# One more seven-product pair per group, more transfers that add, and an instruction order computed by the kernel, in a streaming-encoder layer

## The chip, the cores and the metric

The kernel runs on one core of a Trainium2 chip. The metric is device microseconds (us) of one execution. PE is the engine for matmuls, DVE the vector engine, ACT the one for activations, POOL and SP issue transfers (POOL those that add to what stands at the destination).

## The reference

One layer on 256 tokens of width 2048, all in float32:

```python
x = x + 0.5 * swiglu(rms_norm(x, ffn1_norm), ffn1_w_up, ffn1_w_down)      # D_FF = 5632
proj = rms_norm(x, mix_norm) @ w_in                                      # columns: q f i g, x_b gate_b, gates
y_a = HGRN2 recurrence over (q, f, i), chunkwise, normed, times silu(g)  # 8 heads of 128
y_b = causal conv(4) -> RG-LRU scan, times gelu(gate_b)
x = x + (sigmoid(gate_A) * (y_a @ w_branch_a) + sigmoid(gate_B) * (y_b @ w_branch_b)) @ w_out
x = x + cross_attention(rms_norm(x), rms_norm(mem))                      # 4 heads, 256 memory tokens
x = x + 0.5 * swiglu(rms_norm(x, ffn2_norm), ffn2_w_up, ffn2_w_down)
return rms_norm(x, final_norm)
```

## The kernel before, in words

Every float32 product is made of three: each operand is split into a high part (ACT copies it, rounded, to `h`) and a low part (DVE subtracts, to `l`; `split`, L119), and PE adds high x high, low x high and high x low into one bank of accumulators (`three`, L448). The stationary operand of a matmul is a 128 x 128 piece of activations, the moving one a stretch of weights of 512 (or 256) columns. Weights come as pieces of 128 x 2048, each brought by SP into one of three `raw` buffers and prepared by `prepare` (L195) into one of three `h` and three `l` buffers. One list, `plan`, gives the order of all pieces; `weights` (L165) prepares two pieces ahead.

A feed-forward network (`ffn`, L467) runs over 11 groups of 512 hidden columns. A group takes 8 pieces of up weights, one per pair p of activation blocks, then up to 4 pieces of down weights of earlier groups. A pair's piece holds a 2 x 2 block product, and there are three kinds:

- plain: 8 block products, 24 matmuls of 512 columns; the weights are split as they are.
- fast: 7 block products instead of 8 (a scheme of sums and differences), 21 matmuls. `prepare` makes three differences of the weights on DVE (`td`, L213 to L215), splits three quarters of the piece (`l`, 128 x 1536) and the differences (`tl`, twice 128 x 1024).
- mixed: 8 block products on the sums that the fast pairs of the same group need, 24 matmuls, weights split as in plain. With the kind "added" the low part is made without DVE (`begin_added`, L186): SP brings the piece into the only `own` buffer, ACT writes its negated high part into `l` (L191), and POOL issues a transfer from `own` that adds to `l` (L192).

`ffn_order` (L42) fixes the order: in groups 3 to 10 the pairs go 1, 3, 0, 4, 2, 6, 5, 7, pairs 0 and 6 mixed (added, but for pair 0 of group 3) and the six others fast; the down pieces, plain, follow. At a group's end DVE and ACT gather the accumulators into `ev`, PE turns them by transposes (L491), and they become `hidop`.

In the middle, a generator (`hgrn`, L752) does the recurrence beside the projections: `pump` takes a step or two from it after each projection product. Its small matmuls (`blocks`, L763, from L768, and L788) have 32 or 64 stationary columns instead of 128, and are built 32, 16 or 8 at a time.

The order on each engine is worked out by the framework's scheduler from program order and priorities; only the first pieces are put in order by hand (`in_turn`, L165 to L182), and `tc.issue_after` holds a few groups back.

Of the kernel before, what the change touches and what calls it, by code (L numbers as in the profile page):

```python
# [2 lines left out]

# [10 lines left out]
P = 128  # L14
# [27 lines left out]
def ffn_order():  # L42

    out, down = [("plain", 0, p) for p in range(8)], [("down", 0, 1, c, 0) for c in range(4)]
    for g in range(1, NG):
        if g < 3:  # L50
            out += [(("mixed", "fast")[p % 2], g, p) for p in (0, 1, 2, 3, 5, 4, 7, 6)]
        else:
            out += [("mixed" if p in (0, 6) else "fast", g, p) for p in (1, 3, 0, 4, 2, 6, 5, 7)]
        if g > 2 and g % 2:
            down = [("down", g - 2, 2, c, b) for c in range(4) for b in (g - 2, g - 1)]
        n = 2 if g < 3 else 4
        out, down = out + down[:n], down[n:]
    return out + [("down", NG - 2, 2, c, b) for c in range(4) for b in (NG - 2, NG - 1)]


@with_exitstack
def block_kernel(ctx: ExitStack, tc: tile.TileContext, xT, xin, memT, vec, gfin, bgate, lruw, wu1, wd1, win, wv,
                 wg, wab, wout, wq, wk, wvm, wo, wu2, wd2, out_):
    nc = tc.nc
    pe, dve, act, sp = nc.tensor, nc.vector, nc.scalar, nc.sync

    def pool(name, bufs, **kw):
        return ctx.enter_context(tc.tile_pool(name=name, bufs=bufs, **kw))

# [9 lines left out]
    @contextmanager  # L79
    def scope(**pools):  # L80
        with ExitStack() as inner:
            for name, bufs in pools.items():
                scoped[name] = inner.enter_context(tc.tile_pool(name=name, bufs=bufs, reuse_waits="tile"))
            yield
            scoped.clear()

# [75 lines left out]
    planned = count()  # L162
    in_turn = ExitStack()
# [22 lines left out]
    def begin_added(src):  # L186

        raw = scoped["own"].tile([P, 2048], F32, name="own", tag="own")
        l = lp.tile([P, 2048], F32R, name="l", tag="l")
        sp.dma_start(raw, src)  # L190
        act.activation(l, raw, ACT.Copy, scale=-1.0)  # L191
        nc.gpsimd.dma_start(l, raw, accum_op=ALU.add)  # L192
        return raw, l
# [145 lines left out]

    FFN_POOLS = dict(wide=3, own=1)  # L340

# [62 lines left out]

    BOTH = [2, 4]
    xd = []

    def operand_pairs(src, gain, q, xg, out):

        for a in src:  # L410
# [8 lines left out]
            if 2 * q + i in BOTH:  # L419
                if 2 * q + i == BOTH[0]:  # L420
                    xd.append(slot(F32R, "xd"))
                n = 512 * BOTH.index(2 * q + i)
                less = [xd[-1][:, a:a + 256] for a in (n, n + 256)]
            out.append(((h, l), less))

        def sums(which=((0, "less"), (0, "sums"), (1, "less"), (1, "sums"))):
            s = slot(name="xs")
            for i, ((h, l), less) in enumerate(out):
                a = [xg[:, i * 512 + j * P:][:, :P] for j in range(4)]

                def made(h, l, n, at, terms):
# [3 lines left out]
                    split(h, l, s[:, at:at + n * P])  # L435

                if less and (i, "less") in which:
                    made(*less, 2, 0, lambda o: ((a[0], a[1], ALU.subtract), (a[2], a[3], ALU.subtract)))
# [28 lines left out]
    def ffn(name, pairs, sq, then, begin=(), sums=(), rstds=()):  # L467
# [39 lines left out]
        for at, e in enumerate(order):  # L507
# [3 lines left out]
            if kind != "down":  # L511
# [13 lines left out]
                if ends or last:  # L525
                    if ends or kind == "plain":
# [4 lines left out]
                        if rstd is None:  # L531
                            with tc.issue_after(done["high"]):
                                rstd = sq.rstd_tokens()
                if ends:
# [115 lines left out]
    def to_mix(c, t):  # L650
# [3 lines left out]
        if c == 0:  # L654
            with tc.issue_after(done["residual"]):
                parameters()
        if c == 2:
# [94 lines left out]
    def hgrn(hf):  # L752
# [10 lines left out]
        def blocks(acc, n, pick):  # L763
            for i in range(8):
                g, h = divmod(i, 4)
                for b in range(0, P, 32):
# [6 lines left out]
                          in1=col("eye", 0, 32)[:, None, :].broadcast_to([P, 8, 32]), op=ALU.mult)  # L773
        nc.gpsimd.memset(S[:, :1024], 0.0)
        yield
# [320 lines left out]

    with scope(**FFN_POOLS):
        ffn("ffn2", pairs2, sq4, to_out, late, sums2)


# [91 lines left out]
```

## Time and profile before

| | us |
|---|---|
| median of 3 runs (2442.12 to 2442.47) | 2442.3 |
| the profiled execution | 2442.24 |
| its span on the core | 2440.5 |
| PE busy | 2430.0 |
| DVE busy | 1892.8 |
| ACT busy | 1390.8 |
| PE's waits in all | 1.4 |
| one late group of the second network | 62.09 |

Busy is time in which an engine runs an instruction. Matmuls overlap in the records, so the sum of their durations is more than the time; what one costs is read from its start to the next start. The profile's row for a group of matmuls gives the first start and the time to the end of the last one. Small matmuls and products of plain float32 have two records each.

### The profile page before, as it was taken

Reading aid. Unit: us, or ns where it says so; the run is one execution under the profiler, and the core shown is the slowest. Engines: PE = TensorE matmul, PEld = TensorE weight load, DVE = VectorE, ACT = ScalarE, POOL = GpSimd, SP = SyncE. Lnnn points to the kernel's source line nnn. Section 1 sums busy time; section 2 is a strip of 40 time slices with the busy share of each in tenths; the row PEclk is TensorE's granted clock in tenths of the full one; section 3 lists DMA queues with packets and bytes.
Section 4 is the critical chain, followed back from the end, with each engine's and each line's share of the span. In section 5 each row is a group of like instructions: output and inputs, shape, how many; then the busy total and the mean of one; then the engine's idle time right before and its main releaser. Section 6 shows DMA issues by size and latency. Waiting matters only on the chain.

```text
span 2440.5 us, 30183 instructions
## 1 busy us (share of the span) xinstructions
PE 2430.0 (100%) x12250; PEld 2033.8 (83%) x12250; DVE 1892.8 (78%) x2016; ACT 1390.8 (57%) x1398; POOL 28.3 (1%) x36
## 2 busy tenths in 40 slices
PE   9999999999999999999999999999999999999998
PEld 8888888888888888888888888888888888888887
DVE  6999999999765757577565676556589999999995
ACT  8566666666554454477435554555555666666664
POOL 0000000000000000000000000000000000000000
PEclk9999999999999999999999999999999999999999
DMA  8557777677555545445555555544555677777763
GB/s 296 207 204 243 255 234 236 234 241 239 200 181 192 180 173 179 176 171 217 191 189 186 206 196 190 190 173 155 189 191 185 232 238 234 234 239 241 237 216 151
DMA packets 75020, 507.59 MB, mean 208 GB/s; under 512 B 8320, under 2 KB 8576, under 8 KB 15232
## 3 DMA queue, kind: packets, MB, share of 16 engines
q1 hardware_dynamic: 69840, 473.06, 53.3%
q0 software_dynamic: 4320, 31.46, 6.7%
q8 instruction: 96, 1.57, 0.2%
q10 hardware_dynamic: 720, 1.13, 0.1%
q14 instruction: 44, 0.36, 0.0%
HBM read 472.07 MB, written 2.10 MB: 194 GB/s over the span
## 4 chain that ended last, share of the span: by engine, by line
PE 97%; DVE 1%; ACT 1%; DMA 1%; issue 0%; SPq 0%; ACTq 0%; DVEq 0%
PE acc L451 18%; PE acc L454 18%; PE acc L452 18%; PE acc L231 11%; PE acc L252 8%; PE acc L253 8%; PE acc L255 8%; PE acc L235 6%; PE acc L491 1%; PE acc L391 1%; ACT h L120 0%; PE acc L768 0%; DVE l L121 0%; DMA xf<-xT 0%; PE acc L1051 0%; PE acc L1006 0%
## 5 line engine op out<-in xcount | busy, mean ns | idle before, releaser
L121 DVE TENSOR_TENSOR l<-raw,h 128x2048 fp32r<-128x2048 f32 (+2 forms) x422 | 877.9, 2087 | 364.8 <-ACT h L120 354.7
L120 ACT ACTIVATE h<-raw 128x2048 fp32r<-128x2048 f32 (+2 forms) x422 | 736.7, 1752 | 615.1 <-PE acc L253 206.2
L451 PE MATMUL acc<-h,xh 128*128 128x512 f32 x1280 | 499.0, 391 | 0.4 <-ACT h L120 0.3
L452 PE MATMUL acc<-h,xl 128*128 128x512 f32 x1280 | 496.9, 389 | 0.0
L120 ACT ACTIVATE h<-td 128x1024 fp32r<-128x1024 f32 x224 | 229.7, 1056 | 177.0 <-PE acc L452 130.8
L252 PE MATMUL acc<-h,ops 128*128 128x512 f32 x832 | 326.9, 393 | 0.0
L253 PE MATMUL acc<-h,ops 128*128 128x512 f32 x832 | 324.3, 390 | 0.0
L121 DVE TENSOR_TENSOR tl<-td,h 128x1024 fp32r<-128x1024 f32 x224 | 267.4, 1220 | 31.6 <-ACT h L120 29.0
L451 PEld LDWEIGHTS acc<-h,xh 128*128 128x128 f32 x1280 | 240.3, 188 | 53.2 <-ACT h L120 3.4
L452 PEld LDWEIGHTS acc<-h,xl 128*128 128x128 f32 x1280 | 240.3, 188 | 49.4
L231 PE MATMUL acc<-ops,h 128*128 128x512 f32 x1152 | 277.9, 393 | 0.2
L451 PE MATMUL acc<-h,hidop 128*128 128x512 f32 x704 | 275.7, 392 | 0.0
L452 PE MATMUL acc<-h,hidop 128*128 128x512 f32 x704 | 274.3, 390 | 0.0
L231 PEld LDWEIGHTS acc<-ops,h 128*128 128x128 f32 x1152 | 211.9, 188 | 42.8 <-DVE ops L292 0.9
L454 PE MATMUL acc<-l,xh 128*128 128x512 f32 x832 | 218.3, 389 | 0.0
L255 PE MATMUL acc<-l,ops 128*128 128x512 f32 x832 | 206.1, 390 | 0.0
L454 PE MATMUL acc<-l,hidop 128*128 128x512 f32 x704 | 188.3, 389 | 0.0
L255 PEld LDWEIGHTS acc<-l,ops 128*128 128x128 f32 x832 | 156.2, 188 | 32.4
L454 PEld LDWEIGHTS acc<-l,xh 128*128 128x128 f32 x832 | 156.0, 188 | 32.5
L252 PEld LDWEIGHTS acc<-h,ops 128*128 128x128 f32 x832 | 156.3, 188 | 32.3
L253 PEld LDWEIGHTS acc<-h,ops 128*128 128x128 f32 x832 | 156.3, 188 | 31.6
L454 PEld LDWEIGHTS acc<-l,hidop 128*128 128x128 f32 x704 | 132.2, 188 | 27.5
(220 smaller groups left out, 2347.9 us busy)
## 6 DMA issues: line engine op xcount, KB each, us to landing
raw<-wu SPq DMA_DIRECT2D x142, 1024.0 KB, 4.8
raw<-wd SPq DMA_DIRECT2D x88, 1024.0 KB, 4.8
raw<-win SPq DMA_DIRECT2D x40, 1024.0 KB, 4.8
raw<-wg SPq DMA_DIRECT2D x32, 1024.0 KB, 4.8
own<-wu SPq DMA_DIRECT2D x30, 1024.0 KB, 5.4
l<-own POOLq DMA_DIRECT2D x30, 1024.0 KB, 7.7
raw<-wab SPq DMA_DIRECT2D x16, 1024.0 KB, 4.8
raw<-wout SPq DMA_DIRECT2D x16, 1024.0 KB, 4.8
```

What stands on the lines that cost most here:

```text
L120: done["high"] = act.activation(h, raw, ACT.Copy).ins
L121: dve.tensor_tensor(out=l, in0=raw, in1=h.bitcast(F32), op=ALU.subtract)
L231: pe.matmul(acc, h[:, k * P:(k + 1) * P], xs[k], start=k == 0, stop=False)
L235: done["product"] = pe.matmul(acc[:, :T], l[:, k * P:(k + 1) * P], xs[k][:, :T], start=False, stop=k == KT - 1).ins
L252: pe.matmul(accs[t], x[:, t * P:][:, :P], h[j], start=first and j == 0, stop=False)
L253: pe.matmul(accs[t], x[:, T + t * P:][:, :P], h[j], start=False, stop=False)
L255: done["product"] = pe.matmul(accs[t], x[:, t * P:][:, :P], l[j], start=False, stop=last and j == 3).ins
L391: pe.transpose(accs[m // 2][:, m % 2 * T + t * P:][:, :P], tile[:, t * 512 + m * P:][:, :P], ident)
L451: pe.matmul(acc, ah, bh, start=start, stop=False)
L452: pe.matmul(acc, al, bh, start=False, stop=False)
L454: pe.matmul(acc, ah, bl, start=False, stop=stop)
L491: pe.transpose(acc[:, z * T + t * P:][:, :P], hid[t][:, (2 * y + z) * P:][:, :P], ident)
```

## The change

Three things change at once.

First, in groups 3 to 10 of both networks pair 0 becomes fast, so that only pair 6 is mixed; the order of the pairs becomes 1, 3, 0, 6, 4, 2, 5, 7. The sums for pair 0's activations are made too (`BOTH` gets a 0), in a buffer of a new pool `third`.

Second, of the down pieces that stand in groups 3 to 10, two of the four per group become "added".

Third, the kernel no longer issues its instructions to the framework as it goes. Queue objects record every operation with what it reads and writes (in cells of a tile); `price` gives each a duration; `arrange` walks through a model of the five engines, three times, and at each free engine takes the ready operation that is due first, PE's among them; and `emit` issues all in that order with the framework's scheduler off. Buffers of a pool are taken in program order where there are eight or fewer.

```diff
@@ ffn_order
-            out += [("mixed" if p in (0, 6) else "fast", g, p) for p in (1, 3, 0, 4, 2, 6, 5, 7)]
+            out += [("mixed" if p == 6 else "fast", g, p) for p in (1, 3, 0, 6, 4, 2, 5, 7)]
@@ class Flow
+    def price(self, op):
+        q, kw = op.queue.name, op.kw
+        n = op.out.cells.size if op.out is not None else 0
...
+        elif q == "PE":
+            op.busy = n / 2400 + 0.0134 if n > 128 else 0.108 if n == 128 else 0.058 if n == 64 else 0.04
...
+    def nominal(self):
+        t = 0.0
+        for op in self.ops:
+            op.nominal = t
+            if op.queue.name == "PE":
+                t += op.busy
...
+    def arrange(self):
...
+            for op in cand[e]:
+                r = op.ready
...
+                for x in op.takes:
+                    r = max(r, x.ring.when(op))
+                if op.nominal > reached + AHEAD:
+                    r = 1e18
+                if op.moved:
+                    r = max(r, dma - BACKLOG)
+                if r <= t + 1e-9:
+                    if best is None or op.due < best.due:
+                        best = op
...
+    def emit(self):
...
+        self.nominal()
+        for _ in range(3):
+            self.arrange()
...
+            outer.enter_context(tc.manual_schedule())
+            for op in self.sequence:
...
+                getattr(op.queue.real, op.method)(*map(real, op.args), **{k: real(v) for k, v in op.kw.items()})
@@ plan_ffn
-            kind = "fast" if e[0] == "fast" else "added" if e[0] == "mixed" and e[1:] > (3, 0) else "plain"
+            kind = "fast" if e[0] == "fast" else "plain"
+            if e[0] == "mixed" and e[1] > 2:
+                kind = "added"
+            if e[0] == "down" and 0 < e[1] < NG - 2 and (e[3] + e[4] - e[1]) % 2 == 0:
+                kind = "added"
@@ weights
-            if i == 0:
-                in_turn.enter_context(tc.manual_schedule(engines={sp.engine, act.engine, dve.engine}))
...
-            if i == 7:
-                in_turn.close()
@@ operand_pairs
-    BOTH = [2, 4]
+    BOTH = [0, 2, 4]
...
-    for q, i in ((1, 17), (2, 18)):
+    for q, i in ((0, 22), (1, 23), (2, 24)):
         rest[i] = lambda q=q: sums1[q](((0, "sums"),))
@@ pump
-                with tc.issue_after(done["product"]):
-                    n -= n if next(side[0]) else 1
+                n -= n if next(side[0]) else 1
@@ at the end of block_kernel
+    flow.emit()
```

What this moves is seen in the built programs. In the changed one every row has the line L409, that of `emit`, so the rows are told apart by their tiles.

The first place is PE in the middle, where the HGRN steps run beside the projections. `ops` are the activations, `h` and `l` the halves of the weights, `silu,k` the small matmuls of the recurrence. Before:

```order
L235 MATMUL acc<-ops,l 128x256 x16
L768 MATMUL acc<-silu,k 32x32 x32
L231 MATMUL acc<-ops,h 128x512 x16
L235 MATMUL acc<-ops,l 128x256 x16
L768 MATMUL acc<-silu,k 32x16 x32
L231 MATMUL acc<-ops,h 128x512 x16
```

And in the changed program, at the second kind of block:

```order
L409 MATMUL acc<-ops,l 128x256
L409 MATMUL acc<-silu,k 32x16
L409 MATMUL acc<-ops,h 128x512
L409 MATMUL acc<-silu,k 32x16
L409 MATMUL acc<-ops,l 128x256
L409 MATMUL acc<-ops,h 128x512
L409 MATMUL acc<-silu,k 32x16
L409 MATMUL acc<-ops,l 128x256
L409 MATMUL acc<-silu,k 32x16
L409 MATMUL acc<-ops,h 128x512 x2
```

The 32 small matmuls of a block stood in a row between two whole runs of 16 large ones; now they are dealt out one by one among the large ones of two products. Over the whole program the 432 matmuls of 32 or 64 stationary columns lie in 16 stretches before and in 363 now.

The second place is DVE in a late group of a network, from a fast piece to the group's last ones. `td` are the differences of a fast piece, `l` of 1536 and `tl` its low halves, `l` of 2048 the low half of a plain piece. Before:

```order
L213 TENSOR_TENSOR td<-raw 128x1024
L214 TENSOR_TENSOR td<-raw,td 128x512
L215 TENSOR_TENSOR td<-raw,td 128x512
L121 TENSOR_TENSOR l<-raw,h 128x1536
L121 TENSOR_TENSOR tl<-td,h 128x1024 x2
L121 TENSOR_TENSOR l<-raw,h 128x2048 x3
L536 TENSOR_TENSOR ev<-acc,ev 128x512
```

Now:

```order
L409 TENSOR_TENSOR td<-raw 128x1024
L409 TENSOR_TENSOR l<-raw,h 128x1536
L409 TENSOR_TENSOR tl<-td,h 128x1024
L409 TENSOR_TENSOR td<-raw,td 128x512
L409 TENSOR_TENSOR tl<-td,h 128x1024
L409 TENSOR_TENSOR td<-raw,td 128x512
L409 TENSOR_TENSOR l<-raw,h 128x2048
L409 TENSOR_TENSOR tl<-td,h 128x1024
L409 TENSOR_TENSOR ev<-acc,ev 128x512 x4
L409 TENSOR_TENSOR l<-raw,h 128x2048
```

The three differences no longer stand together, the operations of two neighbouring pieces are dealt into each other, and of the plain pieces at the group's end two are left of four.

The third place is the end of PE's program, the last down piece. The two accumulators (18363 and 18364 before, 18490 and 18516 now) are the two halves of the tokens. Before, behind the first half's last matmul:

```order
L454 MATMUL acc_18363<-l_18359,hidop_18105 128x512 x2
L451 MATMUL acc_18364<-h_18358,hidop_18097 128x512
L452 MATMUL acc_18364<-h_18358,hidop_18097 128x512
...
L454 MATMUL acc_18364<-l_18359,hidop_18097 128x512 x2
L454 MATMUL acc_18364<-l_18359,hidop_18105 128x512 x2
```

Now:

```order
L409 MATMUL acc_18490<-l_18484,hidop_18281 128x512
L409 MATMUL acc_18516<-h_18471,hidop_18276 128x512
L409 MATMUL acc_18490<-l_18484,hidop_18281 128x512
L409 MATMUL acc_18516<-h_18471,hidop_18281 128x512 x4
L409 MATMUL acc_18516<-l_18484,hidop_18276 128x512 x2
L409 MATMUL acc_18516<-l_18484,hidop_18281 128x512 x2
```

The second half had 12 matmuls to itself at the end (8 with the high half of the weights, 4 with the low one); now the two halves are summed in turns and 8 are left to it.

More of the change, by code (lines that the diff above doesn't have):

```diff
@@ new lines, with __init__, reset, when @@
+class Buffer(View):
+    def __init__(self, ring, shape, dt, name):
+        grain = shape[1] if "space" in ring.pool.kw else 1 if shape[1] <= 128 else 32
+        super().__init__(self, np.arange(shape[1]) // grain)
+        self.ring, self.shape, self.dt, self.name = ring, shape, dt, name
+        self.at = self.index = None
+        n = -(-shape[1] // grain)
+        self.writer, self.readers = [None] * n, [set() for _ in range(n)]
+        self.users = []
+        self.left = 0
+class Ring:
+    def __init__(self, pool, tag, bufs):
+        self.pool, self.tag, self.bufs = pool, tag, bufs
+        self.takers = []
+        self.spare = bufs if bufs <= 8 else bufs // 4
+        self.reset()
+    def reset(self):
+        self.free = [(0.0, i, None) for i in range(self.bufs)]
+        self.head, self.taken = 0, set()
+    def when(self, op):
+        if not self.free or self.takers[self.head] is not op and len(self.free) <= self.spare:
+            return 1e18
+        return min(self.free)[0]
+    def take(self, op):
+        f = min(self.free)
+        self.free.remove(f)
+        self.taken.add(op)
+        while self.head < len(self.takers) and self.takers[self.head] in self.taken:
+            self.head += 1
+        return f
@@ L337, in rstd_tokens @@
             return r
-    FFN_POOLS = dict(wide=3, own=1)
+    FFN_POOLS = dict(wide=3, own=1, third=1)
     class TokenSquares:
```

286 lines of the change are left out of this document (266 added, 20 removed).

## The prediction

> **What bounds the kernel now.** I read the page first: busy times, slices, the chain that ended last.
>
> ```profile
> span 2440.5 us, 30183 instructions
> PE 2430.0 (100%) x12250; PEld 2033.8 (83%) x12250; DVE 1892.8 (78%) x2016; ACT 1390.8 (57%) x1398; POOL 28.3 (1%) x36
> ...
> PE   9999999999999999999999999999999999999998
> ...
> DVE  6999999999765757577565676556589999999995
> ...
> PE 97%; DVE 1%; ACT 1%; DMA 1%; issue 0%; SPq 0%; ACTq 0%; DVEq 0%
> ```
>
> PE is busy from end to end and is 97% of the chain; DVE is nearly full in the first and last quarter, the two feed-forward networks. Then the waits of PE:
>
> ```profile
> engine line waited for: us in total, times, longest us
> PE warm L109 <- DVE ones L106: 1.1, 1, 1.1
> PE acc L451 <- ACT h L120: 0.3, 1, 0.3
> ```
>
> PE waits 1.4 us in the whole program. The time is therefore PE's own stream plus a start and an end, and two questions decide: what the stream takes after the change, and whether the other engines still keep ahead of it. For the second, the stages: an early stretch of the first network, and one whole late group of the second.
>
> ```profile
> core 0: us, PE busy (x) PEld busy (x) DVE busy (x) ACT busy (x) POOL busy (x), PEclk, DMA share, GB/s
> 61.00:122.00 61.00, 60.87 (x269) 48.99 (x268) 60.14 (x65) 34.09 (x30) 0.00 (x0) 1.00 0.57 206
> ```
>
> ```profile
> 2055.45:2117.54 62.09, 62.09 (x280) 51.52 (x279) 57.35 (x56) 38.47 (x33) 1.72 (x2) 1.00 0.72 236
> ```
>
> In the late group DVE works 57.35 of 62.09 us: 4.74 us are left. In the early stretch it works 60.14 of 61 and PE still stands only 0.13 us. The granted clock is 1.00 in both.
>
> **The fewer matmuls.** In the groups from the fourth on, pair 0 becomes a "fast" product: 7 products of 3 matmuls instead of 8. That takes 3 matmuls from each of 8 groups of 2 networks, 48 in all; the built order agrees (512-wide matmuls: 9712 before, 9664 now). What one takes in the stream is read from start to start:
>
> ```profile
> 311.68 1.98 PE L454 MATMUL acc<-l,xh 128*128 128x512 f32 x8
> 313.49 0.39 PE L451 MATMUL acc<-h,xh 128*128 128x512 f32 x1
> ```
>
> Eight starts in 1.81 us: 0.2266 us each (the 0.39 is a duration that overlaps the next). 48 x 0.2266 = **10.9 us less**.
>
> **What hides the added operand work.** A fast product costs DVE one 1024-wide and two 512-wide differences, one 1536-wide and two 1024-wide splits; an added one costs DVE nothing, a plain one a 2048-wide split:
>
> ```profile
> 2064.34 2.28 DVE L121 TENSOR_TENSOR l<-raw,h 128x2048 fp32r<-128x2048 f32 x1
> 2066.54 0.68 DVE L563 SCALAR_TENSOR_TENSOR x<-acc,x 128x512 f32<-128x512 f32 x1
> ...
> 2082.94 1.22 DVE L213 TENSOR_TENSOR td<-raw 128x1024 f32<-128x1024 f32 x1
> ...
> 2089.47 1.22 DVE L213 TENSOR_TENSOR td<-raw 128x1024 f32<-128x1024 f32 x1
> ```
>
> Start to start a fast piece takes 6.53 us and a plain split 2.20. Per group, one fast piece more and two plain down pieces fewer: 57.35 + 6.53 - 4.40 = 59.48 us of DVE in a group that PE now does in 62.09 - 3 x 0.2266 = 61.41. The cover is thin, 1.9 us, but the early stretch above ran with 0.9 us. What queues behind DVE when it waits is the next low half (l, tl) that PE needs. ACT and the transfers have more room:
>
> ```profile
> L120 ACT ACTIVATE h<-td 128x1024 fp32r<-128x1024 f32 x224 | 229.7, 1056 | 177.0 <-PE acc L452 130.8 <-DVE td L213 20.4 <-DVE td L215 15.2
> L120 ACT ACTIVATE h<-raw 128x1536 fp32r<-128x1536 f32 x112 | 166.9, 1490 | 159.6 <-issue 94.8 <-PE acc L452 62.9 <-ACT hidop L495 1.6
> L191 ACT ACTIVATE l<-own 128x2048 fp32r<-128x2048 f32 x30 | 57.3, 1910 | 13.8 <-DMA own<-wu 13.8
> ```
>
> ```profile
> own<-wu SPq DMA_DIRECT2D x30, 1024.0 KB, 5.4
> l<-own POOLq DMA_DIRECT2D x30, 1024.0 KB, 7.7
> ```
>
> ACT per group: fast for added is 1.49 + 2 x 1.06 - 2 x 1.91 = -0.2, two down pieces each pay one more 1.91: 38.47 + 3.6 = 42.1 of 61.4. The one `own` buffer carries three pieces per group instead of two, each 5.4 + 1.9 + 7.7 = 15.0 us in a row: 45 of 61.4. Transfers go from 14 to 15 per group, share 0.72 to about 0.77. The sums for pair 0 are made once per network, in the groups ahead. I take 0.25 us of new waits per group, 16 groups: **4 us more**. The ends: nothing, or all 4.74 us of DVE's present idle staying as waits on top of 59.48, so 64.2 instead of 61.4: 2.8 x 16 = 45 us.
>
> **The new order of PE in the middle.** This is the largest term. In the HGRN stage the small matmuls (32 to 64 columns out of 128) stand in 16 solid stretches before. Now each stands alone between two large ones: counting the rows of the built order, the same 432 small matmuls lie in 363 stretches, 308 of them of one. Each is two records on PE. What a stretch costs, at one block of 32 (64 records):
>
> ```profile
> 821.83 0.88 PE L235 MATMUL acc<-ops,l 128*128 128x256 f32 x6
> 822.63 0.74 PE L768 MATMUL acc<-silu,k 128*32 128x16 f32 x64
> 823.30 3.92 PE L231 MATMUL acc<-ops,h 128*128 128x512 f32 x16
> 827.06 2.08 PE L235 MATMUL acc<-ops,l 128*128 128x256 f32 x16
> 828.97 3.82 PE L231 MATMUL acc<-ops,h 128*128 128x512 f32 x16
> 832.63 0.64 PE L235 MATMUL acc<-ops,l 128*128 128x256 f32 x4
> ```
>
> ```profile
> L768 PE MATMUL acc<-silu,k x768: 182/183/217, 804.2 to 988.2; 128*32 128x16 f32 x160, 128*32 128x32 f32 x32
> ```
>
> The 16 at 827.06 take 1.91 us, 0.119 each; so after the 6 at 821.83 the next would start at 822.55, and the small ones start at 822.63: 0.08 on entering. The last small record starts at 822.63 + 0.74 - 0.18 = 823.19, the first large one at 823.30: 0.11 on leaving. And the 16 behind them take 3.76 us to 827.06 where the undisturbed 16 at 828.97 take 3.66: another 0.10. Together **0.29 us per stretch**, whatever is in it; inside, 63 steps take 0.56 us, 0.009 per record. (The edges show no semaphore to explain them: PE has no wait there in the waits above.)
>
> Before: 16 x 0.29 + 848 x 0.009 = 12.3 us. After: 363 x 0.29 + 501 x 0.009 = 109.8 us. **97.5 us more**. The bounds, since the trace has no lone small matmul: below, the price inside a block, nothing at the edges (then even the present 16 edges go, 4.6 us less); above, an entry and an exit each at full price with the wider 64-column kind, about 0.35, 118 us. I take the full 0.29, since in every block the entry is paid by its first matmul and the exit by its last, and a lone one is both.
>
> [...]
>
> The transposes (128 x 128) are broken up too, from 8 in a row into ones and twos. They cost the same either way:
>
> ```profile
> 1556.92 1.07 PE L255 MATMUL acc<-l,ops 128*128 128x512 f32 x4
> 1557.83 0.27 PE L1019 MATMUL acc<-vt,p 128*128 128x128 f32 x1
> 1557.86 0.48 PE L252 MATMUL acc<-h,ops 128*128 128x512 f32 x1
> 1558.17 0.49 PE L1019 MATMUL acc<-vt,p 128*128 128x128 f32 x3
> ```
>
> A lone one takes 1558.17 - 1557.83 - 0.227 = 0.11 us, though the matmul behind it seems to start at once; three starts in a row are (0.49 - 0.27) / 2 = 0.11 apart. Term: nothing, 3 us at most either way.
>
> **Start and end.** The start keeps its chain (transfer, ACT, first product). At the end the last two residual tiles are now summed alternately:
>
> ```profile
> 2429.06 0.69 DVE L563 SCALAR_TENSOR_TENSOR x<-acc,x 128x512 f32<-128x512 f32 x1 [5.93 <-PE acc L454]
> ...
> 2432.32 0.68 DVE L563 SCALAR_TENSOR_TENSOR x<-acc,x 128x512 f32<-128x512 f32 x1
> ...
> 2435.14 0.71 ACT L1093 ACTIVATE x<-x,rtok 128x512 f32<-128x512 f32 x1
> ```
>
> The residual adds of the two halves stand 3.26 us apart, behind 12 matmuls of the second half; in the new order 8 are left there, 1.8 us, and the first half's small operations, which filled the gap, now partly queue with the second half's on DVE and ACT: **1 us more**, between 0 and 2.
>
> **The sum.** The profiled execution took 2442.24 us (span 2440.5, 1.7 around it), as the median 2442.3 does. 2442.3 - 10.9 + 4 + 97.5 + 1 = 2533.9; **2534 us**.
>
> **The rivals.**
> - *A lone small matmul hides its edges* behind the long stream of the matmuls on both sides. Then the small term is -4.6 and the sum 2442.3 - 10.9 - 4.6 + 1 + 0 to 4 = 2428 to 2432, faster. For it: loads of stationary operands are hidden everywhere else (PEld 83% busy beside PE). Against it: at the edges the entry is late by 0.08 and the exit by 0.21 though a large matmul stands there too. It decides at a price of 10.9 / 347 = 0.03 us per stretch: below, the change is a gain.
> - *Half the price*: only one of entry and exit stays. 347 x 0.15 - 3 = 49 more: 2442.3 - 10.9 + 49 + 5 = 2485.
> - *DVE becomes the bound as well*: full edges and 45 us of waits in the 16 groups: 2534 - 4 + 45 = 2575. For it: 1.9 us of cover. Against: the early stretch.
> - That the change doesn't do what it says is excluded by the order: 48 matmuls fewer, 48 added transfers instead of 30.
>
> **How the numbers follow.** Full edges with small waits: 0.62 (2515 to 2555). Half price: 0.16 (2470 to 2515). Full edges and DVE bound: 0.08 (2555 to 2590). Hidden edges: 0.11 (2425 to 2437.4). The rest, 0.03, is a wash within 0.2%, about what a measurement of this kernel can tell from no change. So faster 0.11, same 0.03, slower 0.86. The range reaches into the half price and into the DVE case, 2475 to 2578.
>
> **What would show it.** Right: PE still near 100% busy, the stretch from 700 to 1100 us some 100 us longer with the same matmuls in it, the late group's period near 61.5 us, DVE 59 to 60 of it. Wrong at the largest term: the HGRN stage no longer than before, or small matmuls whose neighbours start 0.23 or 0.12 us apart as if they weren't there. Wrong in the networks: PE waits for DVE's l or tl, or for the transfer into `l`, and periods over 62.1. If the start or the end moves by more than 3 us, my reading of those was wrong.

## The result, and the profile after

| | before | after |
|---|---|---|
| median, us | 2442.2 (2442.06 to 2442.47, 4 runs) | 2580.05 (2575.16 to 2588.14, 4 runs) |
| ratio | 1 | 1.0568 (95%: 1.0536 to 1.0599) |
| the profiled execution, us | 2442.24 | 2576.2 |
| its span, us | 2440.5 | 2574.4 |
| PE's waits in all, us | 1.4 | 7.2 |
| mean granted clock of the profiled execution | 0.999 | 0.996 |

The change costs 137.8 us, 5.7%. The forecast had the sign, the place and the kind of price (by the stretch), but a size of 91.7 us; the time lies 2 us over the upper end of its range. The first part of the page after, then the waits of PE:

```profile
span 2574.4 us, 30356 instructions
PE 2556.9 (99%) x12202; PEld 2065.8 (80%) x12202; DVE 1913.1 (74%) x2088; ACT 1452.5 (56%) x1455; POOL 43.9 (2%) x54
...
DVE  7999999999653444346766566655669999999995
ACT  7566666667543232237844555455555666667664
```

```profile
engine line waited for: us in total, times, longest us
PE acc L409 <- DVE ops L409: 3.0, 2, 1.6
PE acc L409 <- DMA l<-own: 2.2, 2, 1.7
PE warm L409 <- DVE ones L409: 1.1, 1, 1.1
PE acc L409 <- ACT S L409: 0.5, 1, 0.5
PE acc L409 <- DVE tl L409: 0.4, 1, 0.4
```

PE has 48 instructions fewer (12202 for 12250), is busy 127 us longer, and still waits for almost nothing. So no other engine became the bound. (In the chain of work that ended last PE now has 87% of the span and DVE 9%, where it was 97% and 1%; PE's listed waits come to 7.2 us all the same.) DVE and ACT show where the time went: their busy shares fall in slices 11 to 18, which is what a stage looks like in which PE got slower and the others have the same work. The first and the last matmul on the tiles `silu,k`, before (two lines of the code) and after (one line; the column after the count is the duration of one, least, median and most, and then the first and last start):

```profile
L768 PE MATMUL acc<-silu,k x768: 182/183/217, 804.2 to 988.2; 128*32 128x16 f32 x160, 128*32 128x32 f32 x32
...
L819 PE MATMUL acc<-silu,k x16: 270/275/275, 894.5 to 1024.0; 128*128 128x128 f32 x16
```

```profile
L409 PE MATMUL acc<-silu,k x880: 182/203/276, 801.0 to 1155.5; 128*32 128x16 f32 x128, 128*32 128x32 f32 x40, 128*64 128x64 f32 x6, 128*128 128x128 f32 x2
```

From 804.2 to 1024.0 it was 219.8 us, and from 801.0 to 1155.5 it is 354.5: 134.7 us more. About 6.4 of these are large matmuls that now stand there and not elsewhere (31 of 256 columns and 12 of 512); 128 us are the loss. Nearly the whole difference lies in this one stretch. PE in a piece of it, in order of time (start, time to the end of the last one, shape, count):

```profile
1093.30 0.40 PE L409 MATMUL acc<-ops,l 128*128 128x256 f32 x2
1093.53 0.40 PE L409 MATMUL acc<-ops,h 128*128 128x512 f32 x1
1093.76 0.28 PE L409 MATMUL acc<-ops,l 128*128 128x256 f32 x1
...
1094.82 0.40 PE L409 MATMUL acc<-ops,l 128*128 128x256 f32 x2
1095.15 0.24 PE L409 MATMUL acc<-silu,k 128*32 128x16 f32 x2
1095.32 0.50 PE L409 MATMUL acc<-ops,h 128*128 128x512 f32 x1
1095.75 0.24 PE L409 MATMUL acc<-silu,k 128*32 128x16 f32 x2
```

Without small matmuls, 512 after 256 columns costs nothing: the two at 1093.30 take 0.23, the 512 at 1093.53 takes 0.23. With them: the two 256 at 1094.82 should be over 0.24 later, at 1095.06; the lone small matmul (two records) starts at 1095.15, so 0.09 on entering. From its start to the large one behind it are 0.17: 0.05 between its own two records and 0.11 on leaving. That large one then takes 0.43 to the next start instead of 0.23: 0.10 for following, and 0.10 for the next entry. Together 0.09 + 0.17 + 0.10 = **0.36 to 0.37 us per stretch**. Taken over all 363 from the starts of the matmuls: entries 55.8 us (with the "following" of a large one that stands alone between two), inside 20.8, exits 43.0, following 19.9, in sum 139.5 (6.7 of it in 10 stretches at a halved clock, which comes next); before, 14.6 for 16 stretches. The difference is 125 us.

The rest of that stretch's loss is a thing the prediction didn't have at all. Windows of 4 us (the column before the share of the DMAs is the granted clock), and PE's rows in them:

```profile
1098.00:1102.00 4.00, 4.00 (x30) 2.65 (x30) 2.95 (x3) 2.18 (x2) 0.00 (x0) 1.00 0.00 0
1102.00:1106.00 4.00, 4.00 (x22) 2.56 (x20) 0.10 (x1) 0.00 (x0) 0.00 (x0) 0.55 0.76 262
1106.00:1110.00 4.00, 4.00 (x22) 2.38 (x21) 1.66 (x1) 0.38 (x1) 0.00 (x0) 0.50 0.02 4
1110.00:1114.00 4.00, 4.00 (x12) 3.06 (x12) 3.00 (x8) 0.00 (x0) 0.00 (x0) 0.50 0.51 172
```

```profile
1101.55 0.39 PE L409 MATMUL acc<-ops,l 128*128 128x256 f32 x1
1101.86 0.23 PE L409 MATMUL acc<-silu,k 128*32 128x16 f32 x2
...
1106.98 0.58 PE L409 MATMUL acc<-ops,l 128*128 128x256 f32 x1
1107.49 0.30 PE L409 MATMUL acc<-silu,k 128*32 128x16 f32 x4
...
1110.36 6.09 PE L409 MATMUL acc<-h,ops 128*128 128x512 f32 x14
1116.28 2.01 PE L409 MATMUL acc<-l,ops 128*128 128x512 f32 x8
1118.13 2.20 PE L409 MATMUL acc<-h,ops 128*128 128x512 f32 x9
```

Here 256 columns and a small matmul have taken turns for some microseconds, PE is "busy" 4.00 of 4.00, and yet the granted clock drops to a half. It stays there until 1116 and slows what has nothing to do with the small matmuls: 14 matmuls of 512 columns take 5.92 us, 0.42 each, where the 8 at 1116.28 take 1.85, 0.23 each. Span times what the mean clock lacks of 1 is 10 us here (0.004 x 2574.4) and 2 before. The four runs are ordered by it: clock 0.996 in the two of 2575 and 2576 us, 0.992 at 2583.9, 0.990 at 2588.1. So the spread of 13 us goes with the clock, and by this rough sum the halved clock costs about 8 us more than before in the profiled execution and 24 in the slowest. Not all of it belongs to the small matmuls: the trace has another stretch of halved clock, 3.4 us from 709.8, before the first of them, behind 3.4 us in which PE was busy for 1.93 and otherwise stood, waiting for `ops`.

Two late groups of the second network, an ordinary one and the longest, each from the transposes at one group's end to those at the next:

```profile
2143.99:2205.66 61.67, 61.67 (x276) 50.66 (x275) 58.09 (x60) 41.96 (x35) 2.60 (x3) 1.00 0.83 262
2267.39:2329.69 62.30, 61.88 (x276) 50.66 (x275) 58.47 (x61) 42.08 (x35) 2.62 (x3) 1.00 0.81 254
```

Each holds a group's 275 matmuls (267 of 512 columns and 8 transposes) and one that overlaps an edge. A group took 62.09 us before. Over the seven late groups the period is 61.6 to 62.3 us in the second network, 61.8 in the mean, and 61.7 to 63.7 in the first, 62.1 in the mean. DVE works 57.6 to 58.5 us of such a group in the second network, ACT about 42, the transfers have a share of 0.81 to 0.85.

### The profile page after: what moved, and what is told of

Read it like the earlier page. It is cut to its first block, busy times and chain, and to the rows that moved or that the text cites. A ratio compares the mean times of both kernels' runs of the same rounds, so it can differ in the third digit from the quotient of the medians.

```text
span 2574.4 us, 30356 instructions
## 1 busy us (share of the span) xinstructions
PE 2556.9 (99%) x12202; PEld 2065.8 (80%) x12202; DVE 1913.1 (74%) x2088; ACT 1452.5 (56%) x1455; POOL 43.9 (2%) x54
## 4 chain that ended last, share of the span: by engine, by line
PE 87%; DVE 9%; issue 2%; DMA 1%; ACT 1%; ACTq 0%; DVEq 0%
PE acc L409 87%; DVE l L409 2%; DVE td L409 2%; DVE tl L409 2%; DVE ev L409 1%; ACT h L409 1%; DMA own<-wd 1%; DVE x L409 1%; DMA l<-own 0%; PE warm L409 0%; DVE hidop L409 0%; ACT x L409 0%; DVE xs L409 0%; DVE xl L409 0%; DVE ops L409 0%
## 5 line engine op out<-in xcount | busy, mean ns | idle before, releaser
L409 DVE TENSOR_TENSOR l<-raw,h 128x2048 fp32r<-128x2048 f32 (+2 forms) x404 | 829.2, 2056 | 476.4 <-PE acc L409 241.4
L409 ACT ACTIVATE h<-raw 128x2048 fp32r<-128x2048 f32 (+2 forms) x404 | 697.1, 1728 | 599.8 <-PE acc L409 453.2
L409 PE MATMUL acc<-h,xh 128*128 128x512 f32 x1256 | 467.0, 391 | 0.0
L409 PE MATMUL acc<-h,xl 128*128 128x512 f32 x1256 | 446.2, 390 | 0.0
L409 PE MATMUL acc<-h,hidop 128*128 128x512 f32 x1408 | 438.8, 394 | 0.0
L409 PE MATMUL acc<-h,ops 128*128 128x512 f32 x1664 | 426.5, 398 | 0.0
L409 PE MATMUL acc<-ops,h 128*128 128x512 f32 x1152 | 407.0, 411 | 3.0 <-DVE ops L409 3.0
L409 ACT ACTIVATE h<-td 128x1024 fp32r<-128x1024 f32 x256 | 265.4, 1055 | 175.3 <-PE acc L409 73.1
L409 PEld LDWEIGHTS acc<-h,ops 128*128 128x128 f32 x1664 | 310.4, 189 | 63.8
L409 DVE TENSOR_TENSOR tl<-td,h 128x1024 fp32r<-128x1024 f32 x256 | 309.9, 1218 | 10.7 <-ACT h L409 10.4
L409 PEld LDWEIGHTS acc<-h,hidop 128*128 128x128 f32 x1408 | 262.1, 188 | 53.7 <-ACT h L409 1.1
L409 PE MATMUL acc<-ops,l 128*128 128x256 f32 x1152 | 290.0, 298 | 0.0
L409 PEld LDWEIGHTS acc<-h,xh 128*128 128x128 f32 x1256 | 235.6, 188 | 49.8 <-DVE hidop L409 0.8
L409 PEld LDWEIGHTS acc<-h,xl 128*128 128x128 f32 x1256 | 235.8, 188 | 49.4
L409 PE MATMUL acc<-l,hidop 128*128 128x512 f32 x704 | 266.1, 394 | 2.2 <-DMA l<-own 2.2
L409 PEld LDWEIGHTS acc<-ops,h 128*128 128x128 f32 x1152 | 207.4, 188 | 38.2 <-DVE ops L409 3.4
L409 PE MATMUL acc<-l,ops 128*128 128x512 f32 x832 | 235.5, 399 | 0.0
L409 PEld LDWEIGHTS acc<-ops,l 128*128 128x128 f32 x1152 | 207.5, 190 | 17.6
L409 PE MATMUL acc<-l,xh 128*128 128x512 f32 x744 | 213.3, 390 | 0.0
L409 PEld LDWEIGHTS acc<-l,ops 128*128 128x128 f32 x832 | 154.0, 188 | 31.9
L409 DVE TENSOR_TENSOR td<-raw,td 128x512 f32<-128x512 f32 x256 | 175.1, 684 | 0.9
L409 PE MATMUL acc<-tl,xh 128*128 128x512 f32 x512 | 165.7, 393 | 0.7 <-DVE tl L409 0.4
## 6 DMA issues: line engine op xcount, KB each, us to landing
raw<-wu SPq DMA_DIRECT2D x156, 1024.0 KB, 6.6
raw<-wd SPq DMA_DIRECT2D x56, 1024.0 KB, 4.9
l<-own POOLq DMA_DIRECT2D x48, 1024.0 KB, 8.5
raw<-win SPq DMA_DIRECT2D x40, 1024.0 KB, 4.8
own<-wd SPq DMA_DIRECT2D x32, 1024.0 KB, 4.8
raw<-wg SPq DMA_DIRECT2D x32, 1024.0 KB, 4.7
own<-wu SPq DMA_DIRECT2D x16, 1024.0 KB, 5.1
raw<-wab SPq DMA_DIRECT2D x16, 1024.0 KB, 4.7
```

What stands on the lines that cost most here:

```text
L409: getattr(op.queue.real, op.method)(*map(real, op.args), **{k: real(v) for k, v in op.kw.items()})
```

## Experiments

The theory after the result: the loss is the price of 0.36 us for each stretch of matmuls with 32 or 64 stationary columns, times 347 more stretches, and a few us of clock. The rivals: the networks lose it (2), the dealing out of large matmuls and transposes loses it (3), and any tiny matmul between large ones pays, whatever its width (4).

Why the change's order deals the small matmuls out at all stands in its due times: each instruction is due before the next one that depends on it by its own duration and a lag, 0.24 us on PE, and the 32 matmuls of a block, which write one accumulator, are linked in a chain. So two neighbours are due 0.28 us apart though `price` has 0.04 for one (in a block of the kernel before it takes 0.018, two records of 0.009), and large ones that are due in between go first.

### e1: links without lag

```diff
-                lag = op.spent if op.deps is not None and s.deps.get(op, True) is not None else 0
+                lag = 0 if s.deps.get(op, True) is None else op.busy if op.queue is s.queue and op.queue.name == "PE" else op.spent
```

> Edit: in the order's due times a link from one PE instruction to the next one on PE is charged with its duration alone, without the 0.24 us of lag. The 432 small matmuls then lie in 16 stretches again instead of 363, and large matmuls and transposes stand in whole runs. Everything else of the change stays. Theory 1 (each stretch of matmuls with 32 or 64 stationary columns costs about 0.37 us at its two edges, as the changed kernel's trace has it): 347 stretches fewer x 0.37 = 128 us off 2580, and the dips of the granted clock go too, so 2440 to 2452, with the stretch from the first to the last small matmul near 208 us. Theory 2 (the networks lose it: DVE and the transfers that add are late): the time stays above 2550.

Measured: 2433.21 us (2431.58 to 2435.41, 5 runs), ratio to before 0.9963 (0.995 to 0.9975). The stretch of the tiles `silu,k` is back at 219.9 us, and the one to the last matmul of 32 or 64 columns at 208.0, as expected:

```profile
L409 PE MATMUL acc<-silu,k x880: 182/183/275, 802.6 to 1022.5; 128*32 128x16 f32 x128, 128*32 128x32 f32 x40, 128*64 128x64 f32 x6, 128*128 128x128 f32 x2
```

One line takes 147 us off the changed kernel, more than the 128 to 140 expected, and leaves it 9.1 us faster than the kernel before. Theory 2 falls. This is the fastest kernel of the study.

### e2: the networks alone, in the framework's order

```diff
 # the kernel before, with only this of the change:
+            out += [("mixed" if p == 6 else "fast", g, p) for p in (1, 3, 0, 6, 4, 2, 5, 7)]
...
+            if e[0] == "down" and 0 < e[1] < NG - 2 and (e[3] + e[4] - e[1]) % 2 == 0:
+                kind = "added"
...
+    BOTH = [0, 2, 4]
...
```

> Edit: the kernel before with the first two parts of the change only (pair 0 fast, its sums, two of four down pieces added); the order stays the framework's. Theory 1: 48 matmuls of 0.2266 us go, 10.9 us, and the networks wait a few us more: 2431 to 2440. Theory 2 (DVE and the transfers bind in the networks): PE waits in the late groups and the time is above the 2442 of before, up to 2480.

Measured: 2451.28 us (2449.3 to 2451.93, 5 runs), ratio 1.0034 (1.0022 to 1.0047): slower than before, where theory 1 had it faster. PE's waits:

```profile
PE acc L461 <- DMA l<-own: 5.3, 2, 4.0
PE acc L461 <- DVE l L121: 1.3, 1, 1.3
```

The listed waits come to under 9 us, and the 10.9 us of fewer matmuls are gone as well, so they aren't the whole of it. What the two networks take beyond their matmuls at 0.2266 us grows by 20 us, 13 in the first and 7 in the second. The new order is what makes the networks' part pay: with the same pieces it is 18 us faster in e1. That is a cost of the first two parts that the prediction put down at 4 us without asking which order they run in.

### e3 and e6: the dose

e3 drops the lag between small matmuls only (72 stretches), e6 keeps it at every fourth link (148); each has its line in place of e1's:

```diff
+                lag = 0 if s.deps.get(op, True) is None else op.busy if op.queue is s.queue and op.busy < 0.06 else op.spent               # e3
+                lag = 0 if s.deps.get(op, True) is None else op.busy if op.queue is s.queue and op.busy < 0.06 and op.i % 4 else op.spent  # e6
```

> Edit: the same as links without lag, but only between small matmuls. 72 stretches instead of 363; the large matmuls keep the changed kernel's alternation of 512 and 256 columns (674 pairs, 702 before) and the scattered transposes. Theory 1: 291 stretches fewer x 0.37 = 108 us off 2580, 2472, and down to 2460 if the clock's dips go as well. Theory 3 (the alternation of large matmuls and the scattered transposes cost the time): close to 2580.

> Edit: between small matmuls only every fourth link keeps its 0.24 us of lag. 148 stretches. Theory 1, a line through the changed kernel (363) and e3 (72) at 0.37 us each: 2468 + 76 x 0.37 = 2496, between 2488 and 2502 as the clock does or doesn't dip. If the price were not by the stretch but by the small matmul (432 in all kernels), it would stay at one of the two ends.

Measured: e3 2468.3 (2467.38 to 2469.03, 4 runs), e6 2493.42 (2491.97 to 2494.57, 4 runs). Both as theory 1 had it, within 4 us. Both keep the changed kernel's 186 stretches of transposes and nearly all its alternation of large matmuls, so theory 3 is out as the main cause.

### e4, e7 and e10: the same matmuls at full width

```diff
-                    pe.matmul(acc[b:b + 32, i * n:(i + 1) * n], kv[:, h, s], pick(qv[:, h, s]), start=True, stop=True)
+                    pe.matmul(acc[:, i * n:(i + 1) * n], kv[:, h, g * P:(g + 1) * P], pick(qv[:, h, s]), start=True, stop=True)
```

and the like in the other loop; e4 in the changed kernel's order, e7 with e1's line, e10 with e6's.

> Edit: the small matmuls take 128 stationary columns instead of 32 or 64 and write all 128 partitions of their accumulator, in the same order, as many, with as many moving columns (the recurrence's scores are not the reference's then). 363 stretches as in the changed kernel. Theory 1 (the price is that of a change of the stationary width, to 32 or 64 columns and back): the entry and the exit fall to what a lone transpose of 128 columns pays, 0.03 to 0.09, and the time to 2480 to 2515. Theory 4 (the price is that of any tiny matmul of plain float32 between large ones, however wide it is): stays at 2570 to 2590.

> Edit: e1 and e4 together: small matmuls with 128 stationary columns, in 16 stretches (the scores are not the reference's). In e4 a record costs 0.1125 us in a run of several and half of 0.225 when two stand alone. Theory 1 (an edge costs only where the stationary width changes, a full-width record costs its own load of 0.11 wherever it stands): 2433 - 15 + 864 x 0.1125 = 2515, up to 2525; so dealing out or not makes no difference at this width, beyond the 14 us by which e3 lies over e1 for other reasons and the clock's dips. Theory 4 (a tiny matmul of any width pays for standing between large ones): the 347 edges saved in e4's order bring it to 2440 to 2470.

> Edit: e6 and e4 together: 128 stationary columns (the scores are not the reference's), 148 stretches, none of them of 32. Granted clock in e7 was 0.977, falling to half 3 to 6 us into each run of 64 tiny records. Theory 6 (the clock falls when tiny matmuls follow each other for some 3 us without a large one): the runs here are shorter, the clock stays near 0.995 and the time is about 2512 + 14 = 2526, up to 2540. If the clock goes by the share of tiny matmuls over the stage as a whole: near e7, 2560 to 2580.

Measured: e4 2546.74 (2535.01 to 2547.78, 4 runs), e7 2569.51 (2564.37 to 2572.11, 4 runs), e10 2588.6 (2584.64 to 2593.21, 4 runs). None lies where it was expected. Two things were missed. One is the price of the records: e4 pays for every one, as its trace shows.

```profile
1002.95 0.28 PE L409 MATMUL acc<-ops,l 128*128 128x256 f32 x1
1003.07 0.29 PE L409 MATMUL acc<-silu,k 128*128 128x16 f32 x2
1003.21 0.48 PE L409 MATMUL acc<-ops,h 128*128 128x512 f32 x1
1003.53 0.29 PE L409 MATMUL acc<-silu,k 128*128 128x16 f32 x2
1003.66 0.36 PE L409 MATMUL acc<-ops,l 128*128 128x256 f32 x1
```

The entry is gone: the 256 at 1002.95 is over in 0.12. From the small one to the 512 are 0.14, and the 512 takes 0.32, 0.09 too much: 0.23 for two records. The other is the clock, in e7 after an undisturbed run of 256 columns:

```profile
816.86 2.08 PE L409 MATMUL acc<-ops,l 128*128 128x256 f32 x16
818.78 10.32 PE L409 MATMUL acc<-silu,k 128*128 128x16 f32 x64
828.95 5.66 PE L409 MATMUL acc<-ops,h 128*128 128x512 f32 x16
```

Within this block the starts are 0.11 apart for some 33 records and 0.21 for the rest; the 16 of 512 columns then take 5.49 us instead of 3.65. The mean clock is 0.977 in e7 and 0.972 in e10, so span times clock (a rough way to take the clock out, good to 1.3 us since the clock has three digits) compares the orders:

| stretches | kernels | 32 or 64 columns: span x clock | 128 columns: span x clock |
|---|---|---|---|
| 363 | changed; e4 | 2574.4 x 0.996 = 2564.1 | 2545.1 x 0.991 = 2522.2 |
| 148 | e6; e10 | 2492.7 x 0.998 = 2487.7 | 2591.4 x 0.972 = 2518.8 |
| 72 | e3 | 2466.9 x 0.998 = 2462.0 | |
| 16 | e1; e7 | 2433.5 x 0.998 = 2428.6 | 2567.4 x 0.977 = 2508.3 |

From 148 to 363 stretches, these two orders cost 76.4 us at the narrow width, 0.355 per stretch, and 3.4 us at full width, 0.016. From 72 to 148 narrow ones cost 25.7 us, 0.34 each. So the price of dealing out belongs to the narrow width; a full-width tiny matmul pays its 0.11 per record in a block too. Theory 4 falls as it was put. It doesn't follow that a lone tiny matmul is cheap at full width: by the starts a stretch costs 0.30 us in e4 (108.2 over 363) and 0.38 in the changed kernel (139.5 over 363). What the narrow width loses when it is dealt out is its low price in a block.

Where the change of width comes in is seen in the loads of the stationary operands, in the changed kernel and then in e4:

```profile
1095.15 0.14 PEld L409 LDWEIGHTS acc<-silu,k 128*32 128x32 f32 x2
1095.31 0.19 PEld L409 LDWEIGHTS acc<-ops,h 128*128 128x128 f32 x1
```

```profile
1002.96 0.31 PEld L409 LDWEIGHTS acc<-silu,k 128*128 128x128 f32 x2
1003.18 0.19 PEld L409 LDWEIGHTS acc<-ops,h 128*128 128x128 f32 x1
```

In e4 the load of the small one starts 0.11 us ahead of its matmul (1002.96 and 1003.07), beside the 256 columns before it. In the changed kernel the loads at 1095.15 and 1095.31 start with their matmuls (1095.15 and 1095.32). So it is at all 726 changes of width in that trace: the load starts at most 0.003 us ahead, where behind a matmul of 512 columns and the same stationary width it starts 0.22 ahead in the median. Neighbours in a block write to different strips of partitions and start 0.007 us apart, so a change of the strip alone isn't the price. The 0.355 us hold the way in and back and the step between the matmul's own two records; how much of the 0.11 on leaving is the next wide load (a full-width record takes 0.11 in e7's block too) wasn't told apart, and what PE does at a change of width was not shown.

Theory 6 (the clock falls with a run of tiny matmuls of some 3 us) fell too: e10's runs are short, 2 to 10 records with large matmuls between (three have 12 or 18), and its clock is the lowest of all, 0.972. No run was made to find what the clock goes by, and it was not shown; this is what the two kernels' traces have. In the changed kernel's clock records the halved stretches between its matmuls last 3.41 us (from 709.84) and 13.65 us (from 1102.37); a third fall stands behind the last matmul. In the 3.41 us ahead of the first two PE started matmuls of 2560 and 2112 moving columns. The program's time at full clock, cut into windows of 3.41 us (as long as the shorter stretch) from each fall backwards, holds 743 windows without a fall behind them, and none had fewer than 2752. (Matmuls of 512 columns end to end come to about 7700, at 0.2266 us each.) In the kernel before, where the clock falls only behind the last matmul, none of 711 such windows had fewer than 4352. So in these two traces the moving columns tell the windows ahead of a fall from the others, whether the rest was waiting (at 709.84) or tiny matmuls (at 1102.37).

### e5: the order alone

```diff
-            out += [("mixed" if p == 6 else "fast", g, p) for p in (1, 3, 0, 6, 4, 2, 5, 7)]
+            out += [("mixed" if p in (0, 6) else "fast", g, p) for p in (1, 3, 0, 4, 2, 6, 5, 7)]
```

and the kinds and sums of before.

> Edit: the changed kernel with the old networks (pairs 0 and 6 mixed, the four down pieces plain, 30 added transfers); only the order is the computed one, with 363 stretches of small matmuls. Theory 1 (the stretches cost the time): the 48 matmuls come back, 10.9 us, a few us of waits in the networks go: 2583 to 2591. Theory 2 (the networks of the change lose it): near 2442, at most 2460.

Measured: 2581.38 us (2577.96 to 2586.4, 4 runs), 1.3 more than the changed kernel and inside its spread. So the loss is the order's. But the 48 matmuls that came back cost 1.8 us in the profiled spans (2576.2 and 2574.4), not 10.9: in this order, too, the change's networks lose most of what they save. 7 of the missing 9 us lie in the two networks, which take 12.2 us beyond their matmuls in the changed kernel and 5.3 in e5; the halved clock accounts for about 2.

### e8 and e11: the cover of the operand work

e8 is e1 with all down pieces plain; e11 is e1 with a higher price for transfers that add:

```diff
-            if e[0] == "down" and 0 < e[1] < NG - 2 and (e[3] + e[4] - e[1]) % 2 == 0:
-                kind = "added"                                                            # e8
-            op.moved = v.cells.size * 512 / 2 ** 20 * (5.2 if "accum_op" in kw else 2.9)
+            op.moved = v.cells.size * 512 / 2 ** 20 * (6.6 if "accum_op" in kw else 2.9)  # e11
```

> Edit: e1 without the added down pieces (all down pieces plain, their low halves made by DVE). Theory of cover (DVE has 59.5 us of work in a group of 61.4 with them, 63.9 without): PE waits for DVE in the late groups, up to 2.5 us in each of 16, so 2455 to 2473. Rival (DVE's work is no limit, its waits in e1 would cover it): 2430 to 2437.

> Edit: e1 with a price of 6.6 us instead of 5.2 for a transfer that adds, so that the model starts it earlier (from issue to landing it took 8.5 us in the changed kernel, and the model has 5.2 + 1.9). Theory: the 2.8 us that PE waits for l in e1 go, 2430 to 2432. Rival: the wait comes from the one own buffer and stays, 2433, or moves elsewhere.

Measured: e8 2439.94 us (2439.45 to 2440.4, 10 runs), e11 2449.84 us (2448.58 to 2451.48, 7 runs). One late group from transposes to transposes, e1 and then e8 (busy times of PE, PEld, DVE, ACT):

```profile
2006.33:2067.82 61.49, 61.49 (x277) 50.87 (x276) 58.72 (x60) 41.75 (x35) 2.61 (x3) 1.00 0.85 264
```

```profile
2006.38:2068.52 62.14, 62.14 (x277) 50.68 (x276) 62.07 (x62) 38.95 (x33) 0.86 (x1) 1.00 0.65 220
```

Without the added downs DVE is full, 62.07 of 62.14 us, though PE lists fewer waits than in e1 (0.8 us for 3.6, without the one at the start). It is a bound then, but a soft one: 0.65 us in a late group, 6.7 us over the whole program, not the 22 to 40 expected. e11 went the wrong way; PE now waits in more places:

```profile
PE acc L409 <- DMA l<-own: 4.6, 4, 2.2
PE acc L409 <- DVE tl L409: 3.5, 7, 0.8
```

A price nearer to the measured transfer made the order worse by 16.6 us. The listed waits grew by 5.4 us, from 3.6 to 9.0. Of the 14.6 us between the two profiled spans 12.4 lie in the first network; what PE loses there beside the listed waits wasn't settled.

### e9 and e12: transposes and large matmuls

e9 adds the transposes to e3's rule (121 stretches instead of 186); e12 is e1 with the lag left on the transposes (120 instead of 52), each again in that one line:

```diff
+                lag = 0 if s.deps.get(op, True) is None else op.busy if op.queue is s.queue and op.queue.name == "PE" and op.busy < 0.11 else op.spent    # e9
+                lag = 0 if s.deps.get(op, True) is None else op.busy if op.queue is s.queue and op.queue.name == "PE" and op.busy != 0.108 else op.spent  # e12
```

> Edit: as e3, but the links of the transposes (128 x 128) lose their lag too: 121 stretches of transposes instead of 186, the small matmuls in 72 as in e3. Theory 5 (a stretch of transposes costs an entry of 0.09 and 0.09 on the large matmul behind it, less what one more in a run costs: about 0.07 us each): 65 x 0.07 = 4.6 us off e3, 2462 to 2465. The prediction's reading (transposes cost the same in a run or alone): 2467 to 2469.

> Edit: as e1, but the transposes keep the lag in their links: 120 stretches of transposes instead of 52, everything else in whole runs (16 stretches of small matmuls, 512 and 256 columns apart). Theory 5 (a stretch of transposes costs about 0.07 us): 68 x 0.07 = 4.8 us over e1, 2437 to 2439. The prediction's reading (no price): 2432 to 2434. What is then left between this and e9, beyond 56 stretches of small matmuls at 0.36 us (20 us), belongs to the alternation of 512 and 256 columns and to the networks' order.

Measured: e9 2467.13 us (2463.57 to 2469.04, 4 runs), e12 2435.22 us (2433.49 to 2436.83, 8 runs). Both lie between the two readings: 1.2 us for 65 stretches and 2.0 for 68, with ranges that overlap those of e3 and e1. At 0.03 us each, the change's 138 more stretches cost about 4 us. e9 and e12 differ by 31.9 us in the medians and by 29.0 in the profiled spans. Of the 29.0, 20.4 lie in the stretch of the tiles `silu,k` (240.4 us against 220.0), and 56 narrow stretches at 0.355 are 19.9; so the alternation of 512 and 256 columns costs next to nothing in it. The other 9 lie in the networks, in the rest of the middle and at the end. PE's 3 us of waits for `ops` are among them, and about 4 us of alternation: a 512 in front of a 256 takes 0.235 us to the next start instead of 0.227, 703 times in e9 and 154 times in e12.

## Why the prediction was wrong, point by point

- **What bounds the kernel: right.** PE was to stay at its end-to-end work, and its listed waits are 7.2 us of 2574.4.
- **The fewer matmuls: right**, 48, seen in the counts; 10.9 us at 0.2266 each.
- **The operand work: right in kind, 4 us put down.** From the starts of matmuls, the two networks take 1392.9 us before and 1393.2 after, with 7.6 us less of large matmuls in them: 7.9 us of new losses where 4 were put down, 2.6 of them waits for `l` and `tl`. The late group was to take 61.4 us and a quarter of waits, and takes 61.8 and 62.1 in the mean. So two of the prediction's signs of being wrong in the networks showed, in small: the waits, and single periods over 62.1. DVE was forecast at 59.5 and works 57.6 to 58.5. (Its work did grow as forecast: a group's records sum to 60.3 us before and 62.4 after, but more of them overlap.) ACT was forecast at 42.1 and is 42.0, the transfers' share at 0.77 and is 0.82. What the step left out is that the cover depends on the order: 20 us by e2 in the framework's (2451.3 against 2442.3 - 10.9).
- **The new order of PE in the middle: the step that failed, by its size.** "0.29 us per stretch" was read from a block of 64 records and is 0.355 by the dose, 0.37 by the rows. The largest part is the inside, which was carried over from the block: 501 steps of 0.009, 4.5 us, where the rows have 20.8. In a block of 64 records four start 0.007 us apart and the next four 0.03 later, 0.009 per record in the mean; the two records of a lone matmul start 0.055 apart in the mean of 308. The entry came out as 0.08 and is 0.09 to 0.10; exits of the kinds with 32 and 64 moving columns take 0.13 and 0.15 instead of 0.11. Of the 27 us by which the rows exceed the forecast, 14 are the inside, 10 the entries and the following, 3 the exits. 347 x 0.355 = 123 us where 97.5 were forecast (125 by the rows): 26 us of the 46 that the forecast lacks.
- **A term that wasn't there: the clock.** The prediction read 1.00 in the networks and took it for the program. Among the dealt-out small matmuls there is a stretch at half clock: 7 of the clock's 8 us in the profiled execution, and about 24 in all in the slowest.
- **The transposes**: put at nothing, 3 at most; about 4 by e9 and e12. The dealing out of 512 and 256 columns was in no term; it is about 4 us by e9's rows. The trace of the changed kernel bounds both: outside the stretch of the tiles `silu,k` the middle takes 7.8 us more than before beyond its matmuls, with 3.0 us of waits for `ops` and 1.7 of halved clock in it.
- **Start and end: right.** From the second residual add to the end of the span it was 8.2 us (2432.32 to 2440.5); now 9.4 (2564.99 to 2574.4). The add's row:

```profile
2564.99 0.69 DVE L409 SCALAR_TENSOR_TENSOR x<-acc,x 128x512 f32<-128x512 f32 x1 [0.17 <-PE acc L409]
```

- **The rivals.** Hidden edges and half price are excluded by the rows. "DVE becomes the bound as well" was put at 2575, close to the measured time, and is wrong all the same: DVE has 3.6 us or more to spare in a late group and the loss lies elsewhere.

In the profiled execution, then, the parts are: 10.8 us less of matmuls, 128.3 more in the stretch of the tiles `silu,k` (97.5 forecast), 7.9 in the networks (4), 7.8 in the rest of the middle (none), 0.7 behind the last matmul; together 133.9. The 4 us to the median are the other runs, with their lower clock.

## What to carry to other kernels

A price read from a long run is a price for runs: before it is multiplied by a count of lone instructions, ask what a lone one pays that the run averages away. In a list scheduler that works with due times, a latency charged on links between instructions that go in order on one engine is what deals them out; charge the duration there, and keep the latency for links between engines. And when an order changes, look at the granted clock of the new order's stages, not at that of the old ones.

## What the runs showed of the hardware

- A full-width tiny matmul of plain float32 took about 0.11 us per record in a block at full clock (e7), and alone, between large ones, 0.23 us for its two records (e4); a 32-wide one took 0.009 per record in a run (the kernel before) and, with the way in and out, 0.36 us when alone (the changed kernel).
- The load of a stationary operand started ahead of its matmul (0.22 us behind 512 columns, in the median), but not across a change between 128 columns and 32 or 64: at most 0.003 us ahead, 726 times in the changed kernel.
- The granted clock halved (1.00 to 0.50) while the profile has PE busy without a gap, 4.00 of 4.00 us at both clocks: at 1102 us of the changed kernel, and in three of e7's blocks after some 33 to 46 tiny records, 3.6 to 5.1 us (an estimate from the 10.17, 9.48 and 8.79 us that the blocks take, at 0.11 and 0.21 per record). In the changed kernel it was back at 1116.03, after 5.7 us of 512-wide matmuls. The moving columns tell the windows apart in its trace: 2560 and 2112 in the 3.41 us ahead of the two falls between its matmuls, 2752 or more where none followed.
